# A gated attention layer on one core: the later token blocks' sums of squares wait for the first block's last transpose

## The chip, the cores and the metric

The kernel runs on one core of a Trainium2 chip. The time is device microseconds of one execution, median of three runs. Its engines are TensorE (PE: matmuls, and transposes as matmuls against an identity), VectorE (DVE), ScalarE (ACT), GpSimd (POOL) and SyncE (SP), which issues all DMA transfers here. Matmul results go to PSUM banks, from which ScalarE or VectorE must read them before the bank is used again.

## The reference

One layer over 1024 latent tokens and 256 context tokens of width 1024, all in float32:

```
mod_x = silu(c) @ w_ada + b_ada              # shift, scale, gate; the context has its own
h  = rms_norm(x) * (1 + scale) + shift       # sum of squares over a token's 1024 channels
pl = h @ w_in                                # 9248 columns: gla q, k, v, gate, low rank; diff q, k, v, gate; merge gates
la = log_sigmoid(low_rank @ w_dec + b_dec) / 16      # two directions, four heads
a  = chunked gated linear attention, both directions (q, k, v, la)
b  = differential attention with 2-D rotary positions (q, k, v)
out = x + gate * ((sigmoid(m1) * (a @ w1) + sigmoid(m2) * (b @ w2)) @ w_out)
```

## The kernel before

**Tiling.** Tokens come in ten blocks of 128: blocks 0 to 3 are the first half of the latent tokens (`half` 0), 4 to 7 the second, 8 and 9 the context. Channels come in eight tiles `k` of 128. A matmul in near-float32 precision is three matmuls: each operand is split in a high and a low part, and high x high, low x high and high x low are summed in PSUM (`mm3`). So every operand costs a conversion on ScalarE or GpSimd (high) and a subtraction on VectorE (low).

**The prologue** (`prologue`, L535 on) runs while the weights of the modulation arrive:
- `xload` loads a token block; `xnorm` sums its squares on ScalarE (`p`, `sm` <- `g`, L211 like all work of that recorder), turns the sum into a factor on GpSimd (a scale and a power, `sm`), and scales the block on VectorE (`g` <- `g`, `sm`). For blocks above 3 it first waits for the event `ev_md`.
- `ada(0)` and `ada(1)` compute the modulation for channel tiles 0 to 3 and 4 to 7 in the PSUM tiles `gs` and `go`, copy it to SBUF (`md`), transpose it into `gt` and set `ev_sh`. `conv` splits the weights of the second part.
- The main loop takes the halves 0, 1 and 2 in turn. For each channel tile it transposes the half's blocks into one PSUM tile `tp` (there are two) and starts `hblock`: ScalarE evicts `tp` with shift and scale (`p` <- `tp`, `shsc`), GpSimd makes the high part (`h`; for the context `kk`), VectorE the low part.

**After it,** a stream (`job_tr`, `job_nat`) multiplies `h` with blocks of 512 columns of `w_in`. Each result tile of 128 columns by 512 tokens takes 24 matmuls, and such a group is called a job here; `mm` (two) and `ma` (one) are their PSUM tiles. A weight block serves many jobs: the first block the keys of the linear attention, the second its queries. The weights (`raw`, three buffers, two channel tiles each) are split into `w` by ScalarE and VectorE (`wstream`). Between these jobs stand `prep_lr` and `job_lr` (the low-rank columns, tiles `pl` and `l`, products in `gs`, `go`, `gt`) and `job_la`: for two directions and four heads a triple of decay matmuls (`gs`, `go`, `gt` <- `l`), which ScalarE and VectorE evict into `g`; for each pair of heads ScalarE then applies exponential and logarithm (with table loads), VectorE combines, and the result is stored (`d_la`). When all eight are stored, the scans of the linear attention load them back (`glab`, `glaf`, with the keys `gk`) into the SBUF space that the tiles `g` and `l` leave.

**What sets the order.** Engines run their own instruction lists in order. The lists are written by a planner (`Driver`) when the program is built: every piece of work is a generator task that yields a time or an event; the planner keeps a clock for each engine from cost formulas, and resumes tasks by their due time and priority. An event that is set earlier or later thus moves the task's instructions in the lists, and by the shifted clocks those of other tasks too. At run time, semaphores keep only true dependencies, among them the reuse of a buffer.

The events here are `ev_md`, set in `ada(1)` at L650 and awaited in `xnorm` at L547.

Of the kernel before, what the change touches and what calls it, by code (L numbers as in the profile page):

```python
# [245 lines left out]
class Hybrid:  # L246
# [288 lines left out]
    def prologue(self):  # L535
        d, a = self.d, self.a
# [21 lines left out]
        ev_x, ev_md = [Event() for _ in range(10)], Event()  # L558
# [56 lines left out]
        def ada(part):  # L615


            m = 4 if part else 2
            pa = []
            for tg in ("gs", "go"):  # L620
                yield from self.acq(tg)
                pa.append(self.t(tg, [m, 512]))
            for k in range(NK):
                yield ev_w[k, part]
                for x, w in enumerate(ev_w[k, part].w):
                    if part:

                        prods = [(pa[x], self.cs[:, k], w[0]), (pa[x][:2], self.cs[:, k, :2], w[1])][::-1 if k else 1]
                        for y, (o, c, ww) in enumerate(prods):
                            e = self.mm(o, c, ww, k == 0 and y == 0, k == NK - 1 and y == 1)  # L630
                    else:
                        e = self.mm(pa[x], self.col[:, k:k + 9:8], w, k == 0, k == NK - 1)
                        self.rel("w", e)
                        yield AtPE(0)
                if part:
                    self.rel(("w", "pl")[k % 2], e, 4)
                    yield AtPE(0)
            md = []
            for x, tg in enumerate(("gs", "go")):
                yield from self.acq("p")  # L640
                md.append(self.t("p", [m, 512]))
                if x:
                    e = self.dve.tensor_copy(md[x], pa[x])
                else:
                    e = self.act.activation(md[x], pa[x], AF.Copy)
                self.rel(tg, e)
            if part == 0:
                d.spawn(ada(1), prio=-1)
            else:
                d.set(ev_md)  # L650
            yield from self.acq("gt")
            pt = self.t("gt", [P, 2, 4, m])
            for x in range(2):
                yield d.whenpe(md[x])
                for y in range(4):
                    e = self.tr(pt[:, x, y], md[x][:, y * P:(y + 1) * P])
                self.rel("p", e)
            yield self.d.when(pt)
            ss = shsc[part]
            for x in range(2):  # L660
                o = 24 + 8 * x + 4 * part
                e = self.dve.scalar_tensor_tensor(ss[:, x], pt[:, x, :, 0:2], float(x), self.col[
                    :, o:o + 4].unsqueeze(2).to_broadcast([P, 4, 2]), ALU.add, ALU.add)
            if part:
                e = self.dve.tensor_tensor(ss, ss, pt[:, :, :, 2:4], ALU.add)
            self.rel("gt", e)
            d.set(ev_sh[part], e)

        yield from self.consts()
        self.d.spawn(loads(), prio=-2)  # L670
        self.d.spawn(conv(), prio=-2)
        self.d.spawn(ada(0), prio=-1)

        def hblock(k, half, pt):
            ctx = half == 2
            n = 256 if ctx else 512
            s = 1 if ctx else 0
            yield from self.acq("p")
            if not ctx:
                yield from self.acq(f"h{half}", 2)  # L680
            v = self.t("p", [P, n])
            if ctx:
                hi, lo = self.hc[0][k], self.hc[1][k]
            else:
                hi = self.t(f"h{half}", [P, n], F32R)
                lo = self.t(f"h{half}", [P, n], F32R)
                self.hx[0][k][half], self.hx[1][k][half] = hi, lo
            sc = shsc[k // 4][:, :, k % 4, s:s + 1]
            yield self.d.when(pt, shsc[k // 4])
            e = self.act.activation(v, pt[:, :n], AF.Identity, bias=sc[:, 0], scale=sc[:, 1])  # L690
            self.rel("tp", e)
            yield e
            yield self.pool.tensor_scalar(hi, v, 1.0, 0.0, ALU.mult, ALU.add)
            e = self.dve.tensor_tensor(lo, v, hi.bitcast(F32), ALU.subtract)
            self.rel("p", e)
            self.d.set(self.ev_h[k, half], e)
# [5 lines left out]
        for half in (0, 1, 2):  # L702
            idx = [8, 9] if half == 2 else [4 * half + j for j in range(4)]
            for i in idx:
                yield ev_x[i]
            for k in range(NK):
                yield ev_sh[k // 4]
                yield from self.acq("tp")
                pt = self.t("tp", [P, 512])
                for j, i in enumerate(idx):  # L710
                    e = self.tr(pt[:, j * P:(j + 1) * P], xs[i][:, k * P:(k + 1) * P])
                self.d.spawn(hblock(k, half, pt), e)
                yield AtPE(0)
            self.rel("g5", e, len(idx))

# [1939 lines left out]
```

## Time and profile before

| | us |
|---|---|
| median of three runs | 1699.21 (1698.17 to 1699.5) |
| the profiled execution | 1697.12 |
| its span, first to last instruction | 1695.4 |
| TensorE busy / VectorE / ScalarE / GpSimd | 1635.8 / 1203.3 / 818.6 / 636.3 |
| mean granted TensorE clock | 0.993 |

A row of the timeline gives the start, the length, the engine and line, the operation with its tiles (output <- inputs, buffer numbers left out), their shapes and how many follow each other; in brackets the engine's idle time ahead of it and what ended that. A row of the windows gives a stretch, its width, the busy time and number of instructions of PE, weight loads, DVE, ACT and POOL, then the granted clock of TensorE (1.00 is full), the share of the DMA engines in use, and GB/s. A row of the waits gives who waited for whom: total, times, longest.

### The profile page before, as it was taken

The page shows a single profiled execution, that of the slowest core. Times are in us where ns is not written, and L with a number is a line of the kernel's source. Part 1 is how long each engine was busy: PE and PEld are TensorE (multiplying, and loading weights), DVE is VectorE, ACT ScalarE, POOL GpSimd, SP SyncE. Part 2 cuts the span into 40 slices and gives each one's busy share as a digit, 9 for nine tenths or more (in the row PEclk, how much of TensorE's full clock was granted, in tenths as well). Part 3 has the DMA queues.
Part 4 walks back from the last instruction along what each step waited for, and adds up shares of the span by engine and source line. Part 5 has one row for each costly group of instructions (what it writes and reads, how often), then busy time and mean ns, then how long its engine had stood idle before and what let it go on. Part 6 is the DMA issues. An engine that isn't in the chain of part 4 may idle for free.

```text
span 1695.4 us, 24607 instructions
## 1 busy us (share of the span) xinstructions
PE 1635.8 (96%) x8381; PEld 1354.9 (80%) x8381; DVE 1203.3 (71%) x1948; ACT 818.6 (48%) x1633; POOL 636.3 (38%) x651
## 2 busy tenths in 40 slices
PE   8899999999899999999999989999999999999999
PEld 3687887888688878788888868888888888887887
DVE  4763976875936466757777659888888888847694
ACT  4784555453442344343333336675666666642231
POOL 1600552552300012425543525566665566640000
PEclk9999999999999999999999999999999999999999
DMA  8537545653334475457999674353685534157432
GB/s 306 200 134 233 177 124 187 205 154 130 96 116 151 143 242 160 145 180 233 287 299 299 197 201 113 96 137 104 198 259 139 143 109 132 60 168 267 149 100 75
DMA packets 262975, 290.29 MB, mean 171 GB/s; under 512 B 23193, under 2 KB 185921, under 8 KB 262849
## 3 DMA queue, kind: packets, MB, share of 16 engines
q1 hardware_dynamic: 262848, 288.71, 54.9%
q8 instruction: 66, 1.08, 0.3%
q14 instruction: 61, 0.49, 0.1%
HBM read 192.70 MB, written 95.94 MB: 170 GB/s over the span
## 4 chain that ended last, share of the span: by engine, by line
PE 68%; DVE 14%; ACT 5%; POOL 4%; issue 4%; DMA 3%; SPq 1%; ACTq 0%; DVEq 0%; POOLq 0%
PE mm L353 16%; PE mc L353 9%; PE ma L353 8%; PE s L353 6%; PE mb L353 5%; PE gs L353 5%; PE b L353 4%; DVE sm L211 4%; PE go L353 3%; PE gt L353 3%; PE b L379 3%; PE tp L353 2%; DVE e L211 2%; ACT e L211 2%; POOL sm L211 2%
## 5 line engine op out<-in xcount | busy, mean ns | idle before, releaser
L211 DVE TENSOR_REDUCE sm<-s 128x1 f32<-128x1024 f32 (+1 forms) x192 | 197.4, 1038 | 33.2 <-PE s L353 32.6
L353 PE MATMUL mm<-w,h 128*128 128x512 f32 x864 | 215.4, 398 | 3.1 <-DVE gb L211 2.0
L211 ACT ACTIVATE e<-s,sm 128x1280 f32<-128x1280 f32 x128 | 170.0, 1330 | 85.3 <-DVE sm L211 77.3
L211 POOL TENSOR_TENSOR at<-ac,at 128x512 fp32r<-128x512 f32 x128 | 186.1, 1454 | 10.7
L353 PEld LDWEIGHTS mm<-w,h 128*128 128x128 f32 x864 | 159.5, 188 | 37.6 <-DVE gb L211 2.6
L353 PE MATMUL s<-kk,aq 128*128 128x512 f32 (+1 forms) x768 | 174.0, 360 | 6.9 <-ACT e L211 6.9
L353 PE MATMUL mb<-h,wt 128*128 128x512 f32 x624 | 170.7, 404 | 5.9 <-DVE ft L211 3.2
L211 POOL TENSOR_SCALAR at<-ac 128x512 fp32r<-128x512 f32 x128 | 96.9, 757 | 188.8 <-ACT ac L211 184.7
L353 PE MATMUL mm<-h,w 128*128 128x512 f32 x624 | 156.8, 402 | 3.4 <-DVE w L211 1.8
L353 PEld LDWEIGHTS s<-kk,aq 128*128 128x128 f32 x768 | 121.0, 188 | 26.3 <-ACT e L211 10.6
L353 PEld LDWEIGHTS mm<-h,w 128*128 128x128 f32 x624 | 117.4, 192 | 29.9 <-DVE w L211 3.1
L211 DVE TENSOR_TENSOR w<-raw,w 128x512 fp32r<-128x512 f32 (+1 forms) x117 | 88.2, 782 | 60.9 <-ACT w L211 60.8
L353 PE MATMUL b<-at,vv 128*128 128x256 f32 x960 | 129.8, 283 | 1.7 <-DVE at L211 1.2
L353 PEld LDWEIGHTS mb<-h,wt 128*128 128x128 f32 x624 | 109.6, 189 | 26.7 <-DVE ft L211 4.2
L353 PEld LDWEIGHTS b<-at,vv 128*128 128x128 f32 x960 | 121.1, 188 | 7.1 <-POOL at L211 2.3
L211 POOL TENSOR_TENSOR sm<-sm,nhalf 128x8 f32<-128x8 f32 (+3 forms) x78 | 105.8, 1357 | 30.8 <-DVE sm L211 25.4
L211 DVE SCALAR_TENSOR_TENSOR e<-e,sm,e 128x1280 f32<-128x1280 f32 x64 | 112.3, 1755 | 1.2
L353 PE MATMUL mc<-h,wt 128*128 128x512 f32 x480 | 111.5, 392 | 1.6 <-DVE wt L211 1.6
L353 PEld LDWEIGHTS mc<-h,wt 128*128 128x128 f32 x480 | 89.7, 188 | 21.8 <-DVE wt L211 2.5
L211 ACT ACTIVATE ac<-b 128x512 f32<-128x512 f32 x121 | 71.8, 597 | 57.8 <-PE b L379 55.6
L353 PE MATMUL ma<-w,h 128*128 128x512 f32 x384 | 96.6, 396 | 0.4 <-DVE gp L211 0.4
L379 PE MATMUL b<-ident,e 128*128 128x128 f32 x604 | 87.6, 273 | 6.9 <-DVE at L211 3.1
(380 smaller groups left out, 3151.0 us busy)
## 6 DMA issues: line engine op xcount, KB each, us to landing
raw<-in_w_in SPq DMA_DIRECT2D x37, 512.0 KB, 5.0
rb<-in_w_in SPq DMA_DIRECT2D x64, 256.0 KB, 2.9
aq<-d_qT SPq DMA_DIRECT2D x128, 128.0 KB, 4.0
d_kT<-pl SPq DMA_DIRECT2D x40, 256.0 KB, 2.4
d_dv<-pl SPq DMA_DIRECT2D x40, 256.0 KB, 2.1
kk<-d_kT SPq DMA_DIRECT2D x32, 320.0 KB, 4.7
gv<-d_v SPq DMA_DIRECT2D x40, 256.0 KB, 4.7
vv<-d_dv SPq DMA_DIRECT2D x16, 640.0 KB, 6.7
```

Of the source, the lines that this page charges most:

```text
L211: self.ins = f(out, *args, **kw).ins
L353: self.ins = self.nc.tensor.matmul(out, lhsT, rhs, start=start, stop=stop, skip_group_check=more).ins
L379: self.nc.tensor.transpose(out, src, self.ident[:n, :n])
```

## The change

`ev_md` is no longer set when the second part of the modulation has been copied out of PSUM. It is set when the transposes of the first half's last channel tile (`k` = 7, `half` = 0) have been put into TensorE's list. The tasks of blocks 4 to 7, and later of the context blocks, wait for it as before.

```diff
@@ ada
             if part == 0:
                 d.spawn(ada(1), prio=-1)
-            else:
-                d.set(ev_md)
             yield from self.acq("gt")
@@ prologue, main loop
                 for j, i in enumerate(idx):
                     e = self.tr(pt[:, j * P:(j + 1) * P], xs[i][:, k * P:(k + 1) * P])
                 self.d.spawn(hblock(k, half, pt), e)
+                if k == 7 and half == 0:
+                    self.d.set(ev_md)
                 yield AtPE(0)
```

Every engine has the same operations as before. The lists differ from the evictions of the first half's tiles 4 to 7 until the first jobs on the second weight block; after that the order is the same again, but for the PSUM tile (`mm` or `ma`) that a job gets.

First, ScalarE's list at the end of the modulation. `g_115` to `g_118` are the token blocks 4 to 7, `p` <- `tp`, `shsc` the evictions of the first half. Before:

```order
L211 ACTIVATE p_556<-gs_327 4x512
L211 ACTIVATE w_584<-raw_522 128x512
L211 ACTIVATE w_588<-raw_522 128x512
L211 ACTIVATE p_561,sm_562<-g_115_536 128x1024
L211 ACTIVATE p_563,sm_564<-g_116_538 128x1024
L211 ACTIVATE p_603<-tp_593,shsc_189 128x512
L211 ACTIVATE p_613<-tp_598,shsc_189 128x512
L211 ACTIVATE p_565,sm_566<-g_117_540 128x1024
L211 ACTIVATE p_582,sm_583<-g_118_542 128x1024
L211 ACTIVATE p_647<-tp_629,shsc_189 128x512
L211 ACTIVATE p_653<-tp_634,shsc_189 128x512
```

The same place in the change:

```order
L211 ACTIVATE p_556<-gs_327 4x512
L211 ACTIVATE w_576<-raw_522 128x512
L211 ACTIVATE w_580<-raw_522 128x512
L211 ACTIVATE p_594<-tp_584,shsc_189 128x512
L211 ACTIVATE p_597<-tp_589,shsc_189 128x512
L211 ACTIVATE p_617<-tp_611,shsc_189 128x512
L211 ACTIVATE p_627<-tp_622,shsc_189 128x512
L211 ACTIVATE p_637,sm_638<-g_115_536 128x1024
L211 ACTIVATE p_646,sm_647<-g_116_538 128x1024
L211 ACTIVATE p_658,sm_659<-g_117_540 128x1024
L211 ACTIVATE p_660,sm_661<-g_118_542 128x1024
```

All four sums of squares now stand behind all four evictions. GpSimd's and VectorE's shares of both tasks move in the same way, and on TensorE 30 matmuls of the first job stand ahead of the second half's first transposes, where 12 stood.

Second, ScalarE's list where the second weight block is split (`w` <- `raw`), beside the third pair of decay heads. Before, from the eviction of the pair's second head on (`g` <- `gt`):

```order
L211 ACTIVATE g_262_1213<-gt_1222,col 128x256
L211 ACTIVATE p_1243<-ma_1199 128x256
L211 ACTIVATE g_255_1164<-g_255_1164 128x1280
L211 ACTIVATE g_262_1213<-g_262_1213 128x1280
L211 ACT_TABLE_LOAD
L211 ACTIVATE g_255_1164<-g_255_1164 128x1280
L211 ACTIVATE g_262_1213<-g_262_1213 128x1280
L211 ACTIVATE p_1277<-mm_1242 128x256
L211 ACTIVATE w_1288<-raw_567 128x512
L211 ACTIVATE g_274_1305<-gs_1307,col 128x512
```

In the change, from the eviction of that pair's first head on:

```order
L211 ACTIVATE g_257_1207<-gt_1215,col 128x256
L211 ACTIVATE p_1223<-ma_1179 128x256
L211 ACTIVATE p_1257<-mm_1222 128x256
L211 ACTIVATE w_1269<-raw_561 128x512
L211 ACTIVATE w_1279<-raw_561 128x512
L211 ACTIVATE w_1289<-raw_563 128x512
L211 ACTIVATE w_1300<-raw_563 128x512
L211 ACTIVATE w_1310<-raw_607 128x512
L211 ACTIVATE w_1322<-raw_607 128x512
L211 ACTIVATE g_280_1332<-gs_1334,col 128x512
```

The six conversions of the loaded buffers now come ahead of the second head's evictions and so of the pair's exponentials. One decay triple fewer has been done by then, and the last pair of heads follows later.

Third, SP's list ahead of the scans' loads. Before:

```order
L318 DMA d_la_75<-g_295_1398 128x1280
L318 DMA d_q_61<-p_1470 128x512
L318 DMA d_q_62<-p_1498 128x512
L318 DMA glab_1585<-d_la_72 128x10x128
L318 DMA glaf_1587<-d_la_68 128x10x128
L318 DMA gk_1589<-d_k_64 128x1280
L318 DMA d_q_63<-p_1533 128x512
```

In the change:

```order
L318 DMA d_q_63<-p_1525 128x512
L318 DMA d_la_75<-g_305_1463 128x1280
L318 DMA d_q_60<-p_1554 128x512
L318 DMA glab_1585<-d_la_72 128x10x128
L318 DMA glaf_1587<-d_la_68 128x10x128
L318 DMA gk_1589<-d_k_64 128x1280
L318 DMA gq_1591<-d_q_60 128x1024
```

The last decay store (`d_la_75`) and the loads behind it now follow the fourth query product's store (`d_q_63`), where they stood ahead of it; each `d_q` store holds the result of one job.

## The prediction

> **What bounds the kernel now.** I read the page's busy shares and its chain first, then the waits of TensorE by stretch, then the stretches round the place of the change.
>
> ```profile
> PE 1635.8 (96%) x8381; PEld 1354.9 (80%) x8381; DVE 1203.3 (71%) x1948; ACT 818.6 (48%) x1633; POOL 636.3 (38%) x651
> ...
> PE 68%; DVE 14%; ACT 5%; POOL 4%; issue 4%; DMA 3%; SPq 1%; ACTq 0%; DVEq 0%; POOLq 0%
> ```
>
> TensorE is busy 96% of the span and carries 68% of the chain, so a change of order can win only what TensorE idles, or runs at a lower clock, in the stretch that is reordered. The order lists differ only between the second modulation product and the start of the decay scans (45.9 to 173 us here); further on every engine has the same operations in the same order, apart from which PSUM bank a product gets. These are that stretch's parts (width, busy time and count by engine, granted TensorE clock, DMA share, GB/s):
>
> ```profile
> 45.90:60.00 14.10, 10.17 (x48) 8.28 (x48) 9.95 (x17) 13.12 (x28) 10.19 (x16) 0.76 0.74 251
> 60.00:84.00 24.00, 23.21 (x127) 18.46 (x126) 18.19 (x27) 14.39 (x25) 17.76 (x28) 1.00 0.46 154
> 84.00:122.90 38.90, 38.60 (x217) 33.41 (x216) 25.35 (x30) 33.55 (x43) 0.00 (x0) 1.00 0.29 111
> 122.90:140.30 17.40, 14.45 (x53) 10.30 (x52) 12.02 (x18) 13.63 (x20) 0.00 (x0) 0.90 0.64 213
> 140.30:173.00 32.70, 32.70 (x146) 27.02 (x145) 10.85 (x12) 10.60 (x21) 2.72 (x2) 1.00 0.84 257
> ```
>
> Two parts lose time: the first idles 3.9 us and the fourth 3.0 us, and both show a lowered clock. If the clock has only the values 1 and 0.5 there, 0.76 over 14.10 us is 6.8 us at half, and 0.90 over 17.40 us is 3.5 us at half. The waits of TensorE (total us, times, longest):
>
> ```profile
> PE tp L379 <- ACT p L211: 3.5, 1, 3.5
> ...
> PE mm L353 <- DVE w L211: 1.8, 3, 1.1
> PE mm L353 <- ACT w L211: 1.2, 1, 1.2
> PE gt L353 <- DVE kk L211: 0.6, 1, 0.6
> ```
>
> The 3.5 us is the wait that the change addresses: transposes want a PSUM bank that ScalarE has not emptied. The 3.0 us of `w` waits belong to the conversion of the second weight block.
>
> **First place: the first block's evictions.** In the timeline of before (start, length, operation, idle before it):
>
> ```profile
> 45.92 1.10 PE L379 MATMUL tp<-ident,g 128*128 128x128 f32 x8
> 50.53 1.97 PE L379 MATMUL tp<-ident,g 128*128 128x128 f32 x8 [3.51 <-ACT p L211]
> ...
> 55.51 0.86 PE L353 MATMUL ma<-h,w 128*128 128x512 f32 x3
> ...
> 46.58 1.15 ACT L211 ACTIVATE w<-raw 128x512 fp32r<-128x512 f32 x2 [1.97 <-DMA raw<-in_w_in]
> 47.64 1.04 ACT L211 ACTIVATE p<-g 128x1024 bf16<-128x1024 f32 x1
> ...
> 49.71 1.43 ACT L211 ACTIVATE p<-tp,shsc 128x512 f32<-128x512 f32 x2
> ```
>
> ScalarE runs two sums of squares from 47.64 to 49.71, and only then empties the two transposed tiles. From the end of the first eight transposes (47.02) to 55.51, TensorE gets eight transposes and six matmuls done in 8.49 us. The change adds and removes no operation. It moves four squares (1.04 us each), their eight GpSimd instructions and four VectorE scalings behind all four evictions of the first block. The evictions then start at 47.64, since the two conversions ahead of them still wait for the weights. They end near 48.4 and 49.1 (1.43 us for two). So TensorE idles about 1.45 us instead of 3.51. For what follows:
>
> ```profile
> 27.08 3.42 POOL L211 TENSOR_SCALAR h<-p 128x512 fp32r<-128x512 f32 x4 [3.85 <-ACT p L211]
> 27.73 0.69 DVE L211 TENSOR_TENSOR h<-p,h 128x512 fp32r<-128x512 f32 x1 [0.58 <-POOL h L211]
> 49.12 0.55 POOL L211 TENSOR_TENSOR sm<-sm,nhalf 128x1 f32<-128x1 f32 x1
> 49.71 0.75 DVE L211 TENSOR_SCALAR g<-g,sm 128x1024 f32<-128x1024 f32 x1 [1.17 <-POOL sm L211]
> ...
> 53.43 0.88 POOL L211 TENSOR_TENSOR sm<-sm,nhalf 128x1 f32<-128x1 f32 x1
> ...
> 145.76 11.04 PE L353 MATMUL mm<-h,w 128*128 128x512 f32 x48
> ```
>
> A tile's high part comes 0.85 us after its eviction and its low part 0.7 us later: 48.4 + 1.6 = 50.0. At full clock the eight transposes end near 49.75, and six matmuls of 0.23 us (11.04 / 48) end near 51.4: 4.1 us won. If the clock still halves for 3.4 us from about 48.5, as in this trace, the transposes take twice as long and the six matmuls end near 52.4: 3.1 us won. The gap that is left lies under low activity just as before, so I lean to the lower end and take 3.5.
>
> What is late next is the second block. The squares now run from about 50.6 to 54.8. With 0.9 us on GpSimd and 0.75 on VectorE the fourth scaled block is there at 56.5, or 57.0 if the two get in each other's way (the same GpSimd power took 0.55 us alone and 0.88 beside a busy VectorE). Its cover is the 30 matmuls that now stand ahead of the second block's transposes: 50.0 + 30 x 0.23 = 56.9, later still at a lowered clock. So this costs 0 to 0.5 us; without the cover it would cost up to 6.9. The context squares follow until 58.9, ahead of the second block's first eviction; TensorE has the 14 low-rank products (`gs`, 3.2 us) by then and its next transposes only at about 61. Both edits are in the 3.5.
>
> [...]
>
> **Second place: the conversion of the second weight block.** It is moved by the planner, not by the diff's line: with its clock shifted, it puts six conversions ahead of the exponentials of the second pair of decay heads, where before the exponentials came first. In before:
>
> ```profile
> 122.88 0.63 PE L353 MATMUL mm<-h,w 128*128 128x512 f32 x2
> ...
> 129.99 0.60 PE L353 MATMUL gs<-l,l 128*128 128x512 f32 x1
> ...
> 130.77 0.86 PE L353 MATMUL mm<-h,w 128*128 128x512 f32 x3
> ...
> 133.80 6.68 PE L353 MATMUL mm<-h,w 128*128 128x512 f32 x28 [0.24 <-DVE w L211]
> ...
> 119.03 2.44 ACT L211 ACTIVATE g<-g 128x1280 f32<-128x1280 f32 x2
> 123.65 1.68 ACT L211 ACTIVATE w<-raw 128x512 fp32r<-128x512 f32 x3
> ...
> 125.46 2.49 DVE L211 TENSOR_TENSOR w<-raw,w 128x512 fp32r<-128x512 f32 x4
> 127.87 1.49 DVE L211 SCALAR_TENSOR_TENSOR g<-g,g 128x1280 f32<-128x1280 f32 x1
> ```
>
> The first job on these weights has 24 matmuls; 20 lie before 133.80 and four after it, so it lasts from 122.88 to 134.72, 11.84 us. At 0.23 us each it needs 5.52, and the decay products inside it take 0.78 (129.99 to 130.77). Lost: 5.54 us. In the change the conversions begin behind the eviction of the second context product. From there to the job's start stand 48 half-width matmuls (0.12 us each, half of 0.23) and one decay triple: 6.5 us. Six conversions at 0.56 us (1.68 / 3) are through ScalarE 3 us ahead of the job, and VectorE's six low parts at 0.62 (2.49 / 4), with one 1.49 us combination between them, just ahead of it. The last two, for channel tiles 6 and 7, need a load that starts when the first raw buffer comes free, some 4.5 us ahead:
>
> ```profile
> DMA to landing us min/median/max: 4.1/4.5/4.9
> ```
>
> It lands about as the job starts. ScalarE gets to it behind three decay evictions and two half-width ones, none longer than a conversion's 0.56 us, the last of them 1.7 us into the job. Its low parts come 2.9 and 3.5 us into the job; they are needed 4.1 and 4.8 us into it. So the bounds are 5.54 won with nothing left, and 0 if the load or ScalarE is 5 us later. The rows put it near the first; I take 5.0.
>
> **Third place: the start of the scans.** The last decay triple moves from the first job on these weights into the third. The scans' tiles take the SBUF space that the decay tiles leave, so their loads wait for the last decay store:
>
> ```profile
> 140.32 5.60 PE L353 MATMUL ma<-h,w 128*128 128x512 f32 x24
> 172.97 0.38 PE L379 MATMUL gt<-ident,ge 128*128 128x128 f32 x2
> ...
> 142.66 0.36 SPq L318 DMA_DIRECT2D d_la<-g  x1
> 146.96 1.05 SPq L318 DMA_DIRECT2D glab<-d_la  x1
> ...
> DMA to landing us min/median/max: 7.0/7.6/8.1
> ...
> 164.89 3.94 DVE L211 TENSOR_TENSOR_SCAN glab<-gm,glab 128x645 f32<-128x645 f32 x2
> 170.95 0.41 DVE L211 TENSOR_TENSOR ge<-gk,ge 128x256 f32<-128x256 f32 x1
> ```
>
> Before, the last triple's store is issued 12.7 us after the triple (129.99 to 142.66), the load 4.3 us after that, and it lands at about 155, 10 us ahead of the scan. On the same scale of work the triple now stands 12 matmuls into the third job, at 143.1: store at 155.8, load at 160.1, landing at 167 to 168. The scan is 2 to 3 us late. TensorE takes its first product at 172.97, 1.6 us after it was ready at 171.36, and the splits behind the scan are later needed. So the cost is 0.5 to 1.7 us, or 0 if the store lands faster; I take 0.8.
>
> **Sum.** 3.5 + 5.0 - 0.8 is 7.7, with 0.3 for the small `kk` wait, whose products now have other matmuls between them: 8.0 us. The profiled execution has span 1695.4 and time 1697.12, 1.7 us round the span. It becomes 1689.1. That execution is 2.1 us under the median of the three runs, 1699.21; so the median goes to 1691.2. Bounds of the parts: 3.1 to 4.1, 0 to 5.5, and 0 to 1.7 lost: 1689.3 at the best, 1697.8 if the second term is nothing and the third full.
>
> **Rivals.**
> *Only the first place wins.* The raw load of tiles 6 and 7 lands late, or ScalarE reaches the conversions later than I placed them, and the `w` wait stays. For it: three raw buffers and SP's strict order. Against it: about 1.2 us of slack in my placing. With nothing won there and 0.3 lost behind the scans: 1695.7.
> *The second block is late.* Squares, GpSimd and VectorE collide, and TensorE waits 2 to 3 us at its transposes, followed by a half-clock stretch. For it: in before the same GpSimd steps stretch when VectorE is busy. Against it: 30 matmuls of cover. The first term falls to about 0.8: 1693.9.
> *The gain is given back.* A later stage waits for something that did not move with TensorE. Against it: SP's queue waits on engines, which all move. 1698.5.
> *Slower: the scans' loads.* Four loads now stand in one bunch behind the decay store. If they were to land one after the other, each taking the longest landing time of the first kind (8.1 us), the third, the keys, would land 24 us after 160, at 184. They are wanted at 170.95, so 13 us late, with 1.6 us of slack; with half of 3.5 us lost at a lowered clock behind so long a wait, some 13 us lost against 8.8 won: 1703.5. This decides from about 8.8 us of stall on. Against it: the DMA moved 257 GB/s in that stretch, by which three loads of 640 KB take 7.5 us together.
>
> **How the numbers follow.** Forecast 0.61; first place alone 0.17; second block late 0.08; given back 0.08; slower 0.06. A measurement can tell about 0.2%, 3.4 us, from no change, so the edge is 1695.8. The forecast and the late block lie below it with nearly all their weight, first-place-alone with half of its own: faster 0.77. Same: the rest of these and the given-back gain, 0.17. Slower 0.06. The forecast's own range is 1688 to 1694.5, a little past its bounds on the fast side, since three runs of before already differ by 1.3 us. Up to 1696.8 the range takes in most of first-place-alone and leaves out the last two cases; below I go to 1687.
>
> **What would show it.** Right: the squares of blocks 4 to 7 begin at 50 to 51 us; the 3.5 us wait is 1.2 to 1.7 us; the first job on the second weight block has less than 1 us of `w` waits and the clock is 1.00 there; the decay scan begins 5 to 7 us earlier than 164.9. Wrong: a wait of the second block's transposes over 1 us, the `w` waits still near 3 us, or a wait of TensorE behind the scans that was not there.

## The result, and the profile after

| | before | after |
|---|---|---|
| median of four runs, us | 1699.36 (1698.17 to 1700.3) | 1690.74 (1689.64 to 1692.25) |
| ratio, 95% interval | | 0.9950 (0.9933 to 0.9967) |
| profiled execution, us | 1697.12 | 1692.25 |
| its span, us | 1695.4 | 1690.5 |
| mean granted TensorE clock | 0.993 | 0.996 |

The change makes the kernel 8.6 us faster; 8.0 were forecast, and 1691.2 us. The two profiled executions show only 4.9 us of it, because before's was faster than all four of its timed ones and after's is the slowest of its four.

The page of after, busy time and the chain that ended last:

```profile
PE 1631.5 (97%) x8381; PEld 1353.1 (80%) x8381; DVE 1202.9 (71%) x1948; ACT 818.9 (48%) x1633; POOL 638.8 (38%) x651
...
PE 69%; DVE 12%; POOL 4%; ACT 4%; issue 3%; DMA 2%; SPq 0%; ACTq 0%; DVEq 0%; POOLq 0%
```

The work is the same, and so is TensorE's share of the span: 1635.8 of 1695.4 us and 1631.5 of 1690.5 us are both 96.5%, which the pages round to 96 and 97. The stretches of the prediction, in after (width, busy time and count of PE, PEld, DVE, ACT, POOL, then granted clock, DMA share, GB/s):

```profile
45.90:60.00 14.10, 11.48 (x61) 9.02 (x62) 9.26 (x17) 12.54 (x28) 10.46 (x15) 1.00 0.91 294
60.00:84.00 24.00, 22.84 (x127) 18.45 (x126) 15.86 (x24) 14.82 (x26) 18.96 (x28) 1.00 0.39 140
84.00:122.90 38.90, 38.90 (x220) 34.15 (x219) 29.84 (x40) 31.77 (x47) 0.11 (x1) 1.00 0.43 147
122.90:140.30 17.40, 17.40 (x80) 14.37 (x79) 10.27 (x11) 13.90 (x17) 0.00 (x0) 1.00 0.48 172
140.30:173.00 32.70, 32.70 (x149) 26.95 (x148) 20.68 (x28) 19.46 (x41) 3.85 (x5) 1.00 0.85 277
```

The clock is 1.00 in all five, and TensorE has not one idle microsecond from 84 to 173. What it still waits for from 45 to 175 us (total us, times, longest):

```profile
PE tp L379 <- DVE g L211: 1.4, 2, 1.1
PE tp L379 <- ACT p L211: 1.4, 2, 1.1
PE gt L353 <- DVE kk L211: 0.9, 1, 0.9
PE gt L379 <- DVE p L211: 0.5, 1, 0.5
PE gt L379 <- ACT p L211: 0.3, 1, 0.3
```

The 3.5 us behind the evictions is 1.4 now, all `w` waits are gone, and one wait is new: `tp` for `g`, the second block's transposes, 1.4 us. The timeline of TensorE at the places of the prediction:

```profile
46.34 1.09 PE L379 MATMUL tp<-ident,g 128*128 128x128 f32 x8
48.54 1.33 PE L379 MATMUL tp<-ident,g 128*128 128x128 f32 x8 [1.10 <-ACT p L211]
...
51.23 0.86 PE L353 MATMUL ma<-h,w 128*128 128x512 f32 x3
...
58.80 0.77 PE L379 MATMUL tp<-ident,g 128*128 128x128 f32 x5 [1.14 <-DVE g L211]
...
118.85 9.05 PE L353 MATMUL mm<-h,w 128*128 128x512 f32 x39
...
163.64 0.38 PE L379 MATMUL gt<-ident,ge 128*128 128x128 f32 x2
```

The same transposes that began at 45.92 in before begin at 46.34 here; a second profile of the changed kernel has them at 45.58, so this is spread between executions. So from now on I count from these transposes, row start minus row start. The first job on the second weight block begins 72.51 us behind them (before: 122.88 - 45.92 = 76.96), and the `gt` products at which both orders come together 117.30 us behind them (before: 127.05). That is a lead of 9.75 us at the end of the reordered stretch; in the second profile of the changed kernel it is 10.12.

### The profile page after: what moved, and what is told of

It is laid out like the page before. It is cut to its first block, busy times and chain, and to the rows that moved or that the text cites. A ratio compares the mean times of both kernels' runs of the same rounds, so it can differ in the third digit from the quotient of the medians.

```text
span 1690.5 us, 24597 instructions
## 1 busy us (share of the span) xinstructions
PE 1631.5 (97%) x8381; PEld 1353.1 (80%) x8381; DVE 1202.9 (71%) x1948; ACT 818.9 (48%) x1633; POOL 638.8 (38%) x651
## 4 chain that ended last, share of the span: by engine, by line
PE 69%; DVE 12%; POOL 4%; ACT 4%; issue 3%; DMA 2%; SPq 0%; ACTq 0%; DVEq 0%; POOLq 0%
PE mm L353 16%; PE mc L353 9%; PE ma L353 9%; PE s L353 6%; PE mb L353 6%; PE b L353 5%; PE gs L353 4%; DVE sm L211 4%; PE go L353 3%; PE gt L353 3%; PE b L379 3%; DVE e L211 2%; PE tp L353 2%; DVE p L211 2%; ACT e L211 2%
```

## The experiments

The prediction's theory was that two places gain apart from each other: the evictions ahead of the squares, and the conversions of the second weight block ahead of a decay pair's exponentials. Each group of experiments was timed beside runs of the kernel before, whose medians were 1699.05, 1700.23, 1699.93 and 1699.33 us; the ratios are to those.

### The first place alone, by holding the conversions

```diff
@@ the stream of the second weight block, ahead of its conversions
+                if gate and x == NK // 2:
+                    yield self.ev_pair
@@ job_la, behind a pair's logarithms
+                if (e, hh) == (1, 0):
+                    self.d.set(self.ev_pair)
```

> The changed kernel, with the planner's second reordering taken back: the conversions of the second weight block are held until the logarithms of the third decay pair are issued, as they stood before the change. The evictions stay ahead of the squares. Theory (two separate gains, about 3.7 us from the evictions, about 6.0 us from the conversions): the transposes' wait stays at 1.4 us twice, the `w` waits at the first job on the second weight block come back to about 3 us with a half-clock stretch, and the median is 3.0 to 4.0 us below the kernel before. Rival A (the gain is the clock's, which recovers early and lets everything behind run early, so the conversions' place does not matter): about 8.6 us below before. Rival B (what is won early is given back at a later wait): 0 to 1 us below before.

Measured: 1706.77 us, ratio 1.0046 (1.0034 to 1.0058): slower than before by 7.7 us. No theory had that. In its timeline (TensorE, then ScalarE, then TensorE):

```profile
115.81 0.40 PE L353 MATMUL gs<-l,l 128*128 128x512 f32 x1
...
116.25 0.69 ACT L211 ACTIVATE g<-gs,col 128x512 f32<-128x512 f32 x1 [3.45 <-DMA d_k<-p]
120.44 2.43 ACT L211 ACTIVATE g<-g 128x1280 f32<-128x1280 f32 x2
126.52 0.61 ACT L211 ACTIVATE w<-raw 128x512 fp32r<-128x512 f32 x1
...
127.19 1.22 PE L353 MATMUL mm<-h,w 128*128 128x512 f32 x2 [7.85 <-ACT w L211]
```

My edit moved the conversions only. TensorE's decay triples did not go back with them: the triple of the pair's second head stands 18 context matmuls ahead of the job, where the change has 3 and before has 87. So this head is evicted at 116.25. The row blames a store for ScalarE's 3.45 us, but the product that it evicts began at 115.81: this is a wait for TensorE. Exponentials, logarithms and conversions all follow it, and the job waits 7.85 us. The kernel is a mix of both orders and worse than before. It does not tell the two places apart. What it shows is the price of the second place where conversions are late in an order made for early ones.

### The second place alone, by holding the exponentials

```diff
@@ the stream of the second weight block, kernel before
+                if gate and x == NK // 2 + 2:
+                    self.d.set(self.ev_pair)
@@ job_la, ahead of a pair's exponentials
+                if (e, hh) == (1, 0):
+                    yield self.ev_pair
```

> The kernel before, squares still ahead of the evictions, but the exponentials of the third decay pair are held until six conversions of the second weight block are issued, as the change's plan has it. Theory: the 3.51 us wait and its half clock of 6.8 us stay, the `w` waits at the first job on the second weight block go to under 0.5 us with a clock of 1.00 there, and the median is 5 to 6 us below the kernel before; the gains of this run and of the run with the first place alone add up to the whole, 8.6 us. Rival A: under 1 us below before, since the conversions' wait would only move to another place. Rival B (the conversions arrive in time only because the first place shifted the work): 1 to 3 us below before.

Measured: 1701.86 us, ratio 1.0016 (1.0007 to 1.0024), again slower, by 2.8 us. Its rows:

```profile
118.42 4.24 ACT L211 ACTIVATE w<-raw 128x512 fp32r<-128x512 f32 x6 [0.22 <-PE ma L353]
122.55 2.42 ACT L211 ACTIVATE g<-g 128x1280 f32<-128x1280 f32 x2
...
131.17 0.65 ACT L211 ACTIVATE w<-raw 128x512 fp32r<-128x512 f32 x1
...
129.84 0.73 PE L353 MATMUL mm<-h,w 128*128 128x512 f32 x2 [1.60 <-ACT w L211]
```

Six conversions are early, but the last two now stand behind the exponentials, at 129.16 and 131.17, and TensorE waits 2.8 us for them. In the changed kernel the exponentials come behind all eight. So six early conversions of eight did not win here, and this run too was no copy of the change's second place. Both misses have one cause: a hold on one task leaves the rest of the order to the planner.

### Only the squares put back

The whole order of the changed kernel is kept by letting the planner count the squares where the change has them, while they are issued where before had them.

```diff
@@ hblock, half 0, k = 4 and 6
+            for i in (k, k + 1):                     # ScalarE, ahead of the eviction
+                act.activation(sq[i], xs[i], AF.Square, accum_out=ss[i])
             e = self.act.activation(v, pt[:, :n], AF.Identity, bias=sc[:, 0], scale=sc[:, 1])
...
+            for i in (k, k + 1):                     # GpSimd, ahead of the high part
+                pool.tensor_scalar(ss[i], ...); pool.tensor_tensor(ss[i], ..., ALU.pow)
...
+            for i in (k, k + 1):                     # VectorE, ahead of the low part
+                dve.tensor_scalar(xs[i], xs[i], ss[i], None, ALU.mult)
```

> The changed kernel with its whole order kept, TensorE's, the conversions' and the scans' places included; only the four squares of blocks 4 to 7, with their GpSimd steps and scalings, are put back where they stood before the change: two ahead of the first two evictions, two ahead of the next two. Theory (two separate gains): the 3.5 us wait at the transposes and a half clock near 48 us come back, the first job on the second weight block stays free of `w` waits, and the time lies 5 to 6 us below the kernel before, 2.5 to 3.7 us above the changed kernel. Rival (since the two runs with one place alone both came out slower than before, the conversions are only in time when everything ahead of them is): the `w` waits come back and the time is within 1.5 us of before.

Measured: 1693.65 us, ratio 0.9968 (0.9955 to 0.9980). By the ratio that is 5.4 us below before (6.6 between the medians) and 3.1 above the changed kernel, whose interval of 0.9938 to 0.9962 overlaps by a little. Two of its stretches, with the columns of above:

```profile
45.90:60.00 14.10, 10.48 (x41) 8.10 (x42) 10.61 (x18) 11.79 (x26) 10.30 (x15) 0.76 0.87 297
...
122.90:140.30 17.40, 17.40 (x79) 14.38 (x78) 12.94 (x16) 14.01 (x21) 0.00 (x0) 1.00 0.61 210
```

The first place is about as bad as in before (a wait of 2.4 us for the evictions, and the clock 0.76 in both), the second as good as in after. The theory holds and the rival falls: the conversions are in time without the first place. Counted from the transposes, its job begins at 75.52, which is 3.01 us later than in after, and its `gt` products stand at 120.31, 6.74 us ahead of before. From the job's start to these products it takes 44.79 us, exactly as after does, where before takes 50.09.

### Squares one channel tile earlier

```diff
-                if k == 7 and half == 0:
+                if k == 6 and half == 0:
                     self.d.set(ev_md)
```

> The changed kernel with the squares released one channel tile earlier (behind tile 6 instead of 7), so that three of the four evictions stand ahead of them; the planner then puts the conversions back behind the exponentials, as they stood before, with the decay products there as well. Theory (two separate gains): the transposes' wait shrinks to 1 to 2 us, the `w` waits of 2.5 to 4 us and a half clock at the first job on the second weight block return, and the time is 2.5 to 4 us below before. Rival (a gain ahead of the decay stage is lost again in it, because the loads of the second weight block and the stores behind it keep their own time): within 1 us of before.

Measured: 1698.29 us, ratio 0.9991 (0.9982 to 1.0000), 1.5 us below before. The interval, 0 to 3.1 us, takes in the rival's and the lower end of the forecast's, so it decides between neither. Its waits of TensorE from 44 to 190 us:

```profile
PE mm L353 <- DVE w L211: 2.2, 3, 1.1
PE tp L379 <- DVE g L211: 1.5, 1, 1.5
PE mm L353 <- ACT p L211: 1.2, 1, 1.2
PE mm L353 <- ACT w L211: 1.2, 1, 1.2
```

The `w` waits are back, 3.4 us in all, with the planner's old order of conversions. In the first place it is ahead of before by 2.46 us when the job begins (74.50 against 76.96), and 1.95 us at the `gt` products. One character in the condition costs 7 us, and most of that at a place 70 us further on that it doesn't name.

### The clock's share of the first place

The kernel before, with 26 transposes that nobody reads in the gap.

```diff
                 self.d.spawn(hblock(k, half, pt), e)
+                if k == 5 and half == 0:
+                    yield from self.acq("go")
+                    ft = self.t("go", [P, 512])
+                    for j in range(26):
+                        self.nc.tensor.transpose(ft[:, j % 4 * P:j % 4 * P + P], xs[0][:, :P], self.ident)
+                    self.rel("go", e)
                 yield AtPE(0)
```

> The kernel before with the order of every engine kept, and 26 transposes more on TensorE (2.8 us of work that nobody reads) behind the first eight transposes of the late tiles, in the 3.51 us for which it waits for ScalarE. This measures the clock's share of the first place alone. Theory (the gap is what halves the clock): 1.00 near 48 us, the eight transposes and six matmuls behind the wait end about 2 us earlier, and the time is 1.5 to 2.5 us below before. Rival (the clock is halved for another reason, or the splits set the pace there): the same half-clock stretch of 6.83 us or one as long, and the time within 0.7 us of before.

Measured: 1699.60 us, ratio 0.9996 (0.9987 to 1.0004), no change that can be told. Its timeline:

```profile
48.45 3.00 PE L717 MATMUL go<-ident,g 128*128 128x128 f32 x26
51.29 1.05 PE L379 MATMUL tp<-ident,g 128*128 128x128 f32 x8
...
53.84 1.42 PE L353 MATMUL mm<-h,w 128*128 128x512 f32 x5 [1.05 <-DVE h L211]
```

The 6.83 us at half clock are gone, and the eight transposes take 1.05 us instead of 1.97. But TensorE then waits 1.05 us for the low part, which has not become earlier. The job begins 75.65 us behind the transposes, 1.31 us better than before. So of the first place's gain the clock alone brings 1.3 us in the profile; the rest needs the evictions to be early. In whole runs 1.3 us can't be told from none: the interval goes from 0.7 us slower to 2.2 faster. The theory was right on the clock and not on the price.

### Factors in pairs

GpSimd computes two blocks' factors with one pair of instructions; all engines keep their order.

```diff
@@ xnorm, blocks 4 to 7
-            self.rel("p", self.act.activation(sq, xs[i], AF.Square, accum_out=ss))
-            self.pool.tensor_scalar(ss, ss, 1.0 / D, EPS, ALU.mult, ALU.add)
-            yield self.pool.tensor_tensor(ss, ss, self.nhalf[:, 0:1], ALU.pow)
+            act.activation(sq, xs[i], AF.Square, accum_out=s2[:, i % 2:i % 2 + 1])
+            if i % 2:
+                pool.tensor_scalar(s2, s2, 1.0 / D, EPS, ALU.mult, ALU.add)
+                pool.tensor_tensor(s2, s2, self.nhalf[:, 0:2], ALU.pow)
```

> The changed kernel, with the same order of work on every engine, but GpSimd computes the scale factors of token blocks 4 and 5 in one pair of instructions and of 6 and 7 in another, so that it needs two small operations for each pair where it needed four. Theory (a small GpSimd operation beside a 0.75 us scaling of VectorE takes as long as that scaling, so factor and scaling alternate and each block costs 1.47 us): the fourth scaled block comes at 57.0 to 57.5 us instead of 58.74, the 1.4 us wait at the second block's transposes shrinks to 0 to 0.3 us, and the median is 1.0 to 1.4 us below the changed kernel. Rival (ScalarE's evictions behind the context squares, not the factors, set that stretch's end): the wait moves to the next transposes and the time is within 0.4 us of the changed kernel.

> The paired factors of the earlier run once more, in the buffers that the single factors had, so that no constant in SBUF moves by 16 bytes. In the earlier run single matmuls from 400 us on were 1 to 3% apart (120 against 118 ns, 237 against 229), with the same order. Theory (the moved addresses made them slower, the pairing itself gains about 0.5 us at the second block): matmuls of 118 and 229 ns again, and a median 0 to 1.2 us below the changed kernel. [...]

The reason for it, from GpSimd's and VectorE's timeline of after (all of it small factors `sm` and scalings of a block):

```profile
55.05 0.75 DVE L211 TENSOR_SCALAR g<-g,sm 128x1024 f32<-128x1024 f32 x1 [0.72 <-POOL sm L211]
...
55.10 0.75 POOL L211 TENSOR_SCALAR sm<-sm 128x1 f32<-128x1 f32 x1
55.94 0.55 POOL L211 TENSOR_TENSOR sm<-sm,nhalf 128x1 f32<-128x1 f32 x1
...
57.99 0.75 DVE L211 TENSOR_SCALAR g<-g,sm 128x1024 f32<-128x1024 f32 x1 [0.71 <-POOL sm L211]
```

With the pairs, in the second version, whose factors lie where the single ones lay:

```profile
52.57 0.19 POOL L572 TENSOR_SCALAR sm<-sm 128x2 f32<-128x2 f32 x1 [1.31 <-ACT p L566]
...
55.87 1.42 DVE L580 TENSOR_SCALAR g<-g,sm 128x1024 f32<-128x1024 f32 x2 [0.87 <-POOL sm L573]
...
57.29 1.03 PE L388 MATMUL tp<-ident,g 128*128 128x128 f32 x8
```

The GpSimd scale takes 0.19 us with VectorE idle and 0.75 us beside VectorE's 0.75 us scaling. In before it is the same for one block: 0.19 us at 48.85, with VectorE idle, and 0.75 us at 54.39, beside the scaling from 54.34 on. So in after factor and scaling take turns, 1.47 us for each block. In pairs the fourth block is scaled at 57.29 instead of 58.74, and the transposes have no wait of note.

The second version measured 1690.54 us, ratio 0.9947 (0.9933 to 0.9961): the wait is gone, the matmuls are at 118 and 229 ns as the theory has it, and the 0.5 us against the changed kernel's ratio can't be told from none. The first version, with the same order, measured 1695.73 us, 0.9974 (0.9965 to 0.9984), 4 us slower than the changed kernel.

### Sixteen bytes of constants

The only difference of the two paired versions is where the factors lie: in the first, two constants of 8 bytes for each partition had moved what lies behind them. So the changed kernel was run with two such constants that nobody uses (GpSimd sets each to zero once).

```diff
+            if i in (4, 6):
+                self.pool.eng.memset(self.c(f"ssp{i}", [P, 2]), 0.0)
             ss = self.t("sm", [P, 1])
```

> The changed kernel, order unchanged on TensorE, ScalarE, VectorE and the queues, with nothing but two constants of 8 bytes for each partition more in SBUF at the place where the first paired run had them, each set to zero once. Theory (the addresses of what lies behind them make single matmuls slower): matmuls of 120 ns instead of 118 from 1000 us on and 232 to 237 ns instead of 229 from 1510 us on, and 3 to 5 us above the changed kernel. Rival (the first paired run was slow for another reason, its pairing): 118 and 229 ns and within 0.7 us of the changed kernel.

Measured: 1694.59 us, ratio 0.9972 (0.9960 to 0.9985), 3.7 us above the changed kernel's. The stretch from 1554 to 1600 us, the changed kernel first, then with the constants (count, busy, mean ns):

```profile
L353 PE MATMUL mc<-h,wt 128*128 128x512 f32 x203 | 46.6, 391 | 0.0
```

```profile
L353 PE MATMUL mc<-h,wt 128*128 128x512 f32 x199 | 46.6, 395 | 0.0
```

In the same 46.6 us 199 matmuls were done instead of 203. From start to start they take 233 ns in the mean against 229: half of them take 237 or 238 ns, a time that none has in the changed kernel. From 1016 to 1500 us, where most matmuls are shorter, the median of all is 120 ns against 118. From the first score products of the other attention, near 1000 us, to the end both kernels with the shift take 702.9 and 704.2 us, and the other twelve 697.5 to 700.7. The theory holds. Which tile's address it is, and why, was not tried.

### The changed kernel again, and the late waits

> The changed kernel once more, unaltered, so that the others are read beside it and a second profile shows which stretches at half clock come at the same place. Theory (the changed kernel's lead of 9.3 us at 164 us shrinks later at waits on DMA-timed work and at half-clock stretches whose length differs from one execution to the next): median 8 to 9.5 us below before, and the half-clock stretches behind 250 us have other lengths than in the first profile. Rival (the later loss is fixed by the changed order): the same stretches of 6.83, 3.41 and 3.41 us at 265, 422 and 695 us.

Measured: 1691.71 us, ratio 0.9950 (0.9938 to 0.9962), the first result again; by the ratio it is 8.5 us below before (7.3 between the medians), where 8 to 9.5 were forecast. Its half-clock stretches behind 250 us are 6.83 us long at 261.3 and 6.83 at 418.4, where the first profile has 6.83 at 265.0, 3.41 at 422.0 and 3.41 at 695.1. So the places recur and the lengths don't. Behind the `gt` products all kernels have the same order. From there to the first score products of the other attention, some 830 us on, this profile takes 825.8 us, the first one of after 829.4, before 824.9. Over the fourteen profiles of this document it is between 823.4 and 829.4 us, with the first one of after as the longest. So the 4.4 us that the profiled pair seems to give back lie within the spread between executions.

Then 56 transposes that nobody reads were put in front of the two late waits near 260 and 417 us, alone and together with the paired factors.

```diff
+    def busy(self, out, n):
+        for j in range(n):
+            self.nc.tensor.transpose(out[:, j % 4 * P:j % 4 * P + P], self.ident, self.ident)
@@ scores, h = 1, g = 1
                     psc = self.t("gs", [P, 2, 2, 2, 64])
+                    self.busy(psc, 18)
@@ sevens, ahead of its first product
+                    self.busy(pm, 38)
```

> The changed kernel with 56 transposes more on TensorE that nobody reads: 18 (2.0 us) ahead of the score products that wait 2.3 to 3.4 us near 260 us, and 38 (4.1 us) ahead of the first seven-product job's start near 417 us, where TensorE idles 4.5 us in two pieces. All other work and order is the same. In the profiles so far the clock was halved behind both places in every execution, for 3.41 or 6.83 us each. Theory (what was won early is partly given back there, because the clock is decided by the idle time summed over fixed stretches of 3.41 us, from about 1.8 us on): 1.00 behind both places, and 2 to 4 us below the changed kernel. Rival (the half clock there costs nothing, since the work behind it is set by VectorE and ScalarE): within 0.7 us of the changed kernel though the clock is 1.00.

> The changed kernel with both additions: the paired factors of blocks 4 to 7 in the old buffers, and the 56 transposes more at the two late waits. Theory: the two do not touch, so 2.5 to 4.5 us below the changed kernel, near 1687. Rival: as for the run with the transposes alone, within 1 us of the changed kernel.

> The run with both additions once more, unaltered, since its interval (0.9921 to 0.9948) and the changed kernel's (0.9938 to 0.9962) still overlap. If it is faster than the changed kernel, the ratio comes out between 0.992 and 0.9945 again; if not, at 0.995.

Alone: 1690.32 us, ratio 0.9943 (0.9931 to 0.9955), so 1.2 us better by ratio, not 2 to 4, and the intervals overlap. Three stretches, the changed kernel first, then with the transposes:

```profile
255.00:275.00 20.00, 16.51 (x67) 13.46 (x66) 13.67 (x29) 8.27 (x26) 7.51 (x14) 0.83 0.39 142
412.00:432.00 20.00, 15.50 (x62) 12.15 (x61) 15.45 (x21) 8.62 (x17) 9.03 (x4) 0.91 0.47 157
440.00:452.00 12.00, 10.08 (x44) 7.72 (x43) 11.90 (x17) 4.09 (x7) 3.52 (x2) 1.00 0.24 69
```

```profile
255.00:275.00 20.00, 18.18 (x90) 15.15 (x90) 14.33 (x30) 9.53 (x30) 7.91 (x15) 0.91 0.42 150
412.00:432.00 20.00, 19.37 (x105) 16.41 (x105) 15.42 (x20) 9.12 (x18) 9.05 (x4) 1.00 0.43 150
440.00:452.00 12.00, 8.76 (x33) 6.77 (x31) 11.89 (x17) 4.08 (x7) 3.50 (x2) 0.86 0.26 78
```

At 417 the clock is 1.00, as forecast; at 260 it is 0.91 over 20 us, so one half stretch is left. What TensorE wins at 417 it waits for again from 440 on, where VectorE is busy 11.9 of 12 us in both, and there the clock now falls to 0.86. Both rival and theory have a part of it.

Together with the paired factors: 1688.89 us, 0.9935 (0.9921 to 0.9948), and once more 1686.68 us, 0.9933 (0.9919 to 0.9947). Its eleven runs against the nine of the changed kernel are 2.4 us faster in the mean, with an interval of 0.7 to 4.2 us; the forecast was 2.5 to 4.5. This is the fastest version here, by little. The two additions' shares can't be told apart.

## Why the prediction was right, and where not

**The mechanism, two places that add up, was right.** Squares put back cost 3.1 us of whole runs, so the first place is worth about that and the second with the rest 5.4, each with 2 to 3 us either way. They were forecast at 3.5 and 5.0.

**First place: 3.5 forecast, about 3.0 measured.** In the profile the eight transposes and six matmuls are done at 51.23 instead of 55.51, 4.28 us earlier, where the prediction had 4.1 for a full clock and 3.1 for a halved one. The second block's wait of 1.4 us takes part of it back. With the squares put back the job begins 3.01 us later, and that is what the first place is worth there. The job's whole lead of 4.45 us has decay triples in it as well, which the prediction's first term did not have: one fewer stands ahead of the job (0.58 us), and before's first and sixth took 0.69 and 1.27 us (the sixth from 110.59 to 111.86), where each of after's takes 0.58. The rest of the first place's wait is 1.10 us, where 1.45 was forecast. The step that failed in part is the lean towards a clock that still halves once: it stayed at 1.00, with 1.11 us of idle time in that stretch of the clock's grid, 46.54 to 49.95 us (last section). That is chance in part. In eight of the nine profiles with all four evictions in front it stayed at 1.00 there; in the ninth, with the paired factors, where the gaps there are 0.92 us and some shorter ones, it halved for 3.41 us at 48.3.

**The second block's scaled tiles: 56.5 to 57.0 forecast, at a cost of 0 to 0.5 us.** They came at 58.74 and TensorE waited 1.4 us. This is the mis-sized term. I had added 0.9 us of GpSimd and 0.75 of VectorE to the last square, as if the four blocks' chains overlapped; they take turns, 1.47 us for each. A wait over 1 us at these transposes was named as a sign of being wrong, and the paired run shows the cause. It cost little: with the wait gone, whole runs are 0.5 us faster by the ratio, which can't be told from none. In the profiles the `gt` products stand 115.6 us behind the transposes with the pairs (116.6 in the one whose clock halved near 48 us) and 116.5 to 117.3 without them, which is 0.9 to 1.7 us.

**Second place: 5.0 forecast, 5.4 measured.** (The pair of heads is the third; the prediction calls it the second.) In the profile after wins 5.30 us between the job's start and the `gt` products, with one decay triple more in this part. The job's 24 matmuls take 5.49 us from its start to the next job's, where before took 11.97 with the 0.78 of a triple among them: 5.70 us won. Behind the job both are alike, 38.1 us without the triples. ScalarE's rows in after:

```profile
113.31 4.23 ACT L211 ACTIVATE w<-raw 128x512 fp32r<-128x512 f32 x6 [0.22 <-PE ma L353]
...
120.39 1.18 ACT L211 ACTIVATE w<-raw 128x512 fp32r<-128x512 f32 x2
...
122.88 2.44 ACT L211 ACTIVATE g<-g 128x1280 f32<-128x1280 f32 x2
```

Six conversions are done 1.3 us ahead of the job at 118.85, not 3; the last two begin 1.5 us into it, where 1.7 was forecast; the exponentials follow all eight. No `w` wait is left. The profile's 5.70 is a little above the bound of 5.54, which counted before's last four matmuls at 0.92 us; they took 1.05. The term of 0.3 for `kk` was no gain: that wait is 0.9 us in after and 0.6 in before.

**Third place: 0.8 forecast, nothing lost.** These are the rows of after:

```profile
146.52 0.36 SPq L318 DMA_DIRECT2D d_la<-g  x1
...
148.51 0.83 SPq L318 DMA_DIRECT2D glab<-d_la  x1
...
155.56 3.94 DVE L211 TENSOR_TENSOR_SCAN glab<-gm,glab 128x645 f32<-128x645 f32 x2
```

The store stands where I had it (155.8 on before's scale, less the 9.33 us of lead at `gt`, is 146.5). But the load follows it by 2.0 us, where I had carried over before's 4.3, and it landed 6.4 us after its issue, not 7 to 8:

```profile
DMA to landing us min/median/max: 6.4/6.4/6.4
```

Together that is about 3 us, the delay that I had forecast. The scan is 9.33 us earlier than in before; I had said 5 to 7.

**The sum: 8.0 forecast, 8.6 measured.** That these are so near is partly luck. The profile's lead of 9.75 us is 3.0 for the first place, 5.7 for the second, and 1.0 for the decay triples (all eight take 5.64 us in before and 4.64 in after), which the sum did not have. The sum had 0.5 more for the first place and 0.7 less for the second, and took off 0.8 and added 0.3 for two effects that did not come.

**The rivals.** First place alone, second block late by 2 to 3 us, and the scans' loads one after the other did not happen. Of the rival that the gain is given back, medians bear out 8.6 of the 9.75 us won by 164 us. The microsecond between them is within the spread of the later stages, and whether it is more than spread stays open.

## What to carry to other kernels

A gap of one engine is worth its length (3.51 us here), plus what the clock loses behind it (6.83 us at half clock here), less what the next chain isn't ready for (1.4 us here); work out that next chain as a queue with its resources and not as one item's latency. Where a planner sets the order, most of an edit's effect can lie at a place that the edit doesn't name, and another edit that shifts the planner's clock a little can lose it again: compare the whole order lists. To test one part, keep the entire order and put back that part alone; holding a task back makes a third kernel, and here both of those were slower than before.

## What the runs showed of the hardware

**The halved clock and the idle time ahead of it.** The clock's records in before and after have the values 1 and 0.5 alone. In every profile all half-clock stretches start on one grid: in before at 48.51, 127.02, 273.79 and 427.39 us, which are 23, 43 and 45 times 3.413 us apart, in after at 264.99, 422.01 and 695.07, 46 and 80 times 3.413 us apart. They last 3.41 or 6.83 us in both (but for the last one, at the program's end: 3.68 and 0.79 us). The grid's offset differs from execution to execution: it is 0.72 us from the span's start in before and 2.17 in after. I summed TensorE's idle time in each stretch of the grid over the fourteen profiles, from 12 us on, where the record of the clock has begun in all. Of 6601 stretches at full clock with under 1.0 us of idle time none was followed by a halved one, of 73 with 1.0 to 1.4 us one was, of 61 with 1.4 to 1.8 us 12, of 49 with 1.8 us or more 46. In before and after alone it was 0 of 941, 0 of 16, 1 of 8 and 6 of 6. Ahead of the halved stretch at 127.02 the gaps were 0.29 and 1.12 us, ahead of the one at 273.79 1.47 and 0.36. (Ends of matmuls are modelled, so these sums are rough.) From these counts I estimate that two gaps of 1 us cost 3.41 us at half clock if they fall into one stretch, and mostly nothing if they don't; no run tested just that. It may be one part of the run-to-run spread: over 150 runs, each beside the mean of its own kernel, a longer time goes with a lower granted clock (correlation 0.65).

**A 16-byte shift in SBUF** made many matmuls late in the kernel slower (half of those between 1554 and 1600 us took 237 or 238 ns, where all took 225 to 232), and the kernel 3.7 us; nothing else had changed but two small operations that set the constants to zero. The first paired version, which had such constants, had this in its time too: 199 matmuls in those 46.6 us.

**A small GpSimd operation** (the scale of one block's factor) took 0.75 us beside a VectorE scaling, just as long as that scaling, and 0.19 us with VectorE idle: 54.39 and 48.85 us in before, and 0.75 us at 55.10 in after.
